# A dilated 3x3 convolution on one core: the first pair of images loaded in one transfer, casts two groups ahead, and stores and a load moved in the queue

## The chip, the core and the metric

The kernel runs on one core of a Trainium2 chip. The metric is device time in microseconds (us) of one execution, lower is better; the median of several runs is given. A profile was taken of one execution. Its engines are PE (matrix products), DVE (vector), ACT (scalar), POOL, and SP, whose queue here issues every transfer between the chip's main memory and the on-chip buffers; the transfers themselves run on 16 DMA engines.

## The reference

Sixteen images of 64 channels and 64x64 pixels (f32) are convolved with a 3x3 kernel of dilation 2 into 128 output channels, with zero padding of 2, so that the output is again 64x64.

```
x: (16, 64, 64, 64) f32      weight: (128, 64, 3, 3) f32      output: (16, 128, 64, 64) f32
output[b, co] += weight[co, ci, kh, kw] * x_pad[b, ci, kh*2 : kh*2+64, kw*2 : kw*2+64]   for all ci, kh, kw
```

So 16.8 MB are read and 33.6 MB are written.

## The kernel before

**Tiles.** The images are taken in pairs: two images of 64 channels fill the 128 partitions, 16 KB of f32 to a partition, 2048 KB to a pair. There are `npairs` = 8 pairs. A pair is worked through in `NG` = 4 groups of 16 rows, so the main loop (L174) runs over 32 groups; `G` counts them all, `pb` is the pair, `g` the group within it. The output of a pair is two images of 2048 KB, kept in one tile `osb` until it is stored.

**Arithmetic.** Rows are grouped by twos, and with dilation 2 the sum over the three kernel rows is rearranged so that two blocks of output share one product. Five kinds of derived weights (`w_sb`, made from `w32` by casts, differences and transposes through PE in `turn`, L116) are used. In each group PE makes three PSUM results: `psP` from `xs` (sums of neighbouring row blocks, 6 matmuls), `psA` and `psB` from `x16` (12 matmuls each). ACT copies `psP` to `p_sb` (L201), and DVE adds `p_sb` to `psA` and to `psB` into `osb` (L206).

**Staging.** `load(pb)` (L60) queues a transfer of a pair into an `x32` tile, of which there are 3. `cast(c)` (L67) is ACT's conversion of one group's rows to f16 (`x16`, 2 tiles of a pair each); it takes rows up to two past its group, since the group's products read two rows ahead. `rowsum(c)` (L77) is DVE's making of `xs`. `osb` has 3 tiles, `p_sb` 3, PSUM one buffer for `psP` and three that `psA` and `psB` share.

**Order.** The order on each engine is the program's: nothing is rescheduled. On SP's queue stand the weights (L86), pair 0 in four pieces (rows 0 to 10, 10 to 18, 18 to 34 and 34 to 64, L87), pairs 1 and 2, and then, from the loop, `load(3)` after group 0 and the two stores of pair 0 after group 3, `load(4)` after group 4, the stores of pair 1 after group 7, and so on. `load(pb + 3)` has to wait until the last cast of pair `pb` has freed the `x32` tile. A wait on SP holds up everything behind it on that queue. The last pair is stored in half images after groups 1 and 3 (L216).

**Ahead of the loop** the rows of group 0 are cast by hand: rows 0 to 10 by ACT (L132), rows 10 to 18 by DVE (L135), then `rowsum(0)` (L139). Between them stand the copies of the five transposed weight kinds from PSUM to `w_sb`: DVE L131, ACT L138, DVE L142, ACT L143, DVE L144. In the loop, `cast(G + 1)` stands after the matmuls of `psP` (L187) and `rowsum(G + 1)` after ACT's copy (L202).

Of the kernel before, what the change touches and what calls it, by code (L numbers as in the profile page):

```python
# [10 lines left out]
def kernel(  # L11
# [9 lines left out]
    B, CI, H, W = x.shape  # L21
# [5 lines left out]
    d = 2  # L27
# [8 lines left out]
    GR = 16  # L36
    NG = H // GR
    NBLK = GR // 4
    NH = GR // 2 * W
    npairs = B // 2  # L40
    ngroups = npairs * NG
# [18 lines left out]
    def load(pb, cuts=(0, H)):  # L60
        x32_tiles[pb] = fpool.tile([P, HW], f32, tag="x32", name="x32")
        for lo, hi in zip(cuts[:-1], cuts[1:]):
            nc.sync.dma_start(  # L63
                out=x32_tiles[pb][:, lo * W : hi * W], in_=x_pair[pb, :, lo * W : hi * W]
            )

    def cast(c):  # L67
        pb, g = divmod(c, NG)
        lo, hi = chunk_rows[g]
        if g == 0:  # L70
            x16_tiles[pb] = xpool.tile([P, HW], f16, tag="x16", name="x16")
            xs_tiles[pb] = xpool.tile([P, HW // 2], f16, tag="xs", name="xs")
        nc.scalar.copy(  # L73
            out=x16_tiles[pb][:, lo * W : hi * W], in_=x32_tiles[pb][:, lo * W : hi * W]
        )

    def rowsum(c):  # L77
        pb, g = divmod(c, NG)
        v = x16_tiles[pb][:, g * GR * W : (g + 1) * GR * W].rearrange(
            "p (b e q) -> p b e q", e=2, q=2 * W  # L80
        )
        s = xs_tiles[pb][:, g * NH : (g + 1) * NH].rearrange("p (b q) -> p b q", q=2 * W)
        nc.vector.tensor_tensor(out=s, in0=v[:, :, 0], in1=v[:, :, 1], op=add)  # L83

    w32 = wpool.tile([CO, CI * KH * KW], f32, name="w32")
    nc.sync.dma_start(out=w32, in_=weight.rearrange("o i h w -> o (i h w)"))  # L86
    load(0, (0, 10, GR + d, 2 * GR + d, H))  # L87
    load(1)
    load(2)
    zero = wpool.tile([P, 512], f16, name="zero")  # L90
# [55 lines left out]
    def product(ps, src, kind, blk0, nblk, first, last):  # L146
        for j in (1, 0, 2):
            dw = (j - 1) * d
            o0, o1 = max(0, -dw), W - max(0, dw)
            t = kind * KW + j  # L150
            for hb in range(2):
                pp = slice(hb * CI, (hb + 1) * CI)
                rhs = src(pp, dw + o0, dw + o1)
                po = ps[:, hb * NH + blk0 * 2 * W : hb * NH + (blk0 + nblk) * 2 * W]
                po = po.rearrange("p (r w) -> p r w", w=W)[:, :, o0:o1]
                nc.tensor.matmul(  # L156
                    out=po,
                    lhsT=w_sb[pp, t * CO : (t + 1) * CO],
                    rhs=rhs,
                    start=first and j == 1,  # L160
                    stop=last and j == 2,
                )

    def blocks(x16, b0, n, e):
        v = x16.rearrange("p (b e r w) -> p b e r w", e=2, r=2, w=W)
        return lambda pp, c0, c1: v[pp, b0 : b0 + n, e, :, c0:c1]

    def store(pb, m, r0=0, r1=H):
        nc.sync.dma_start(
            out=out_img[2 * pb + m, :, r0 * W : r1 * W],  # L170
            in_=o_tiles[pb][:, m * HW + r0 * W : m * HW + r1 * W],
        )

    for G in range(ngroups):  # L174
        pb, g = divmod(G, NG)
        x16 = x16_tiles[pb]
        xs = xs_tiles[pb].rearrange("p (r w) -> p r w", w=W)
        if g == 0:
            o_tiles[pb] = opool.tile([P, 2 * HW], f32, tag="osb", name="osb")
        o = o_tiles[pb].rearrange("p (m b e q) -> p m b e q", m=2, e=2, q=2 * W)  # L180
        b0 = g * NBLK

        psP = ppool.tile([P, 2 * NH], f32, tag="p", name="psP")
        sv = lambda pp, c0, c1: xs[pp, g * GR // 2 : (g + 1) * GR // 2, c0:c1]
        product(psP, sv, 0, 0, NBLK, True, True)

        if G + 1 < ngroups:  # L187
            cast(G + 1)

        psA = apool.tile([P, 2 * NH], f32, tag="ab", name="psA")  # L190
        product(psA, blocks(x16, b0, NBLK, 1), 1, 0, NBLK, True, False)
        z = 1 if g == 0 else 0
        product(psA, blocks(x16, b0 + z - 1, NBLK - z, 1), 2, z, NBLK - z, False, True)

        psB = apool.tile([P, 2 * NH], f32, tag="ab", name="psB")
        product(psB, blocks(x16, b0, NBLK, 0), 3, 0, NBLK, True, False)
        z = 1 if g == NG - 1 else 0
        product(psB, blocks(x16, b0 + 1, NBLK - z, 0), 4, 0, NBLK - z, False, True)

        p_sb = spool.tile([P, 2 * NH], f32, tag="psb", name="p_sb")  # L200
        nc.scalar.copy(out=p_sb, in_=psP)  # L201
        if G + 1 < ngroups:  # L202
            rowsum(G + 1)
        pv = p_sb.rearrange("p (m b q) -> p m b q", m=2, q=2 * W)
        for e, ps in ((0, psA), (1, psB)):
            nc.vector.tensor_tensor(  # L206
                out=o[:, :, b0 : b0 + NBLK, e],
                in0=ps.rearrange("p (m b q) -> p m b q", m=2, q=2 * W),
                in1=pv,
                op=add,  # L210
            )

        if g == NG - 1 and pb < npairs - 1:
            store(pb, 0)
            store(pb, 1)
        if g % 2 == 1 and pb == npairs - 1:  # L216
            store(pb, 0, (g - 1) * GR, (g + 1) * GR)
            store(pb, 1, (g - 1) * GR, (g + 1) * GR)
        if g == 0 and pb + 3 < npairs:
            load(pb + 3)  # L220


# [33 lines left out]
```

## Time and profile before

| | us |
|---|---|
| median of 5 runs (128.08 to 130.51) | 129.08 |
| the profiled execution, its time | 129.52 |
| its span, from first to last instruction | 127.7 |
| last instruction of DVE ends | 109.5 |
| PE, DVE, ACT busy | 104.6, 91.2, 65.1 |

A page of the profile gives the busy time of each engine, the load of the DMA engines in 40 equal slices of the span, the chain of work that ended last, the costliest groups of instructions and the DMA issues. Besides it the trace answers questions: a table by stretches of time (busy time of each engine, granted PE clock, share of the 16 DMA engines, GB/s), a timeline of instructions, waits by engine, and the landing times of transfers. "L156" is line 156 of the kernel.

### The profile page before, as it was taken

To read this page: it belongs to the slowest core of one execution; us is meant where nothing else is said; L and a number is where in the kernel's file an instruction comes from. 1 tells how busy PE (TensorE), PEld (TensorE's weight loads), DVE (VectorE), ACT (ScalarE), POOL (GpSimd) and SP (SyncE) were. 2 spreads that over 40 slices of the span, in tenths; PEclk is the share of its full clock that TensorE was granted. 3 is DMA by queue.
4 is the path that set the end of the run, shared out by engine and by line. 5 is a ranking of instruction groups with operands and counts; after the bars stand their busy time and mean duration, and the time that the engine had idled before them with its cause. 6 is when DMAs were issued, how large, how long until landed. Compare 5 with 4: busy or idle time off the path is not lost.

```text
span 127.7 us, 2334 instructions
## 1 busy us (share of the span) xinstructions
PE 104.6 (82%) x996; PEld 48.4 (38%) x996; DVE 91.2 (71%) x103; ACT 65.1 (51%) x68; POOL 2.2 (2%) x8
## 2 busy tenths in 40 slices
PE   6669999999999999999999999999999998000000
PEld 2324444444444444444444544444444443000000
DVE  0556888988898889888888988898889887300000
ACT  4555566656665666566656665665666533000000
POOL 2400000000000000000000000000000000000000
PEclk9968999999999999999999999999999999975555
DMA  4999999999999999999999999999999999999980
GB/s 140 274 403 460 431 410 421 395 416 446 364 369 323 426 436 423 426 421 441 426 421 428 431 431 421 436 431 431 426 431 426 431 426 431 426 413 421 426 341 21
DMA packets 4330, 50.78 MB, mean 398 GB/s; under 512 B 480, under 2 KB 480, under 8 KB 1120
## 3 DMA queue, kind: packets, MB, share of 16 engines
q1 hardware_dynamic: 4320, 50.63, 95.7%
q8 instruction: 8, 0.13, 0.4%
q14 instruction: 2, 0.02, 0.0%
HBM read 17.07 MB, written 33.55 MB: 396 GB/s over the span
## 4 chain that ended last, share of the span: by engine, by line
PE 78%; DMA 4%; DVE 2%; DVEq 1%; SPq 1%; issue 0%
PE psA L156 32%; PE psB L156 30%; PE psP L156 17%; DMA x<-in_x_dram 4%; DVE osb L206 1%; DVEq L251 1%; DVE x L135 0%; DVE xs L83 0%; SPq L63 0%; SPq L86 0%; DVEq L206 0%; DVEq L83 0%
## 5 line engine op out<-in xcount | busy, mean ns | idle before, releaser
L156 PEld LDWEIGHTS <-w_sb 64*128 64x128 f16 x960 | 46.7, 95 | 55.1 <-issue 1.9
L201 ACT COPY p_sb<-psP 128x1024 f32<-128x1024 f32 x32 | 32.4, 1012 | 36.5 <-issue 31.9
L206 DVE TENSOR_TENSOR osb<-psA,p_sb 128x1024 f32<-128x1024 f32 x32 | 39.2, 1225 | 12.6 <-PE psA L156 11.8
L156 PE MATMUL psA<-x,w_sb 64*128 64x496 f16 (+3 forms) x384 | 45.5, 371 | 0.0
L156 PE MATMUL psB<-x,w_sb 64*128 64x496 f16 (+3 forms) x384 | 44.5, 365 | 0.0
L206 DVE TENSOR_TENSOR osb<-psB,p_sb 128x1024 f32<-128x1024 f32 x32 | 39.1, 1222 | 0.0
L73 ACT CAST x<-x 128x1024 f16<-128x1024 f32 (+2 forms) x31 | 32.4, 1044 | 0.3 <-DMA x<-in_x_dram 0.3
L156 PE MATMUL psP<-xs,w_sb 64*128 64x496 f16 (+1 forms) x192 | 26.1, 379 | 1.3 <-DVE xs L83 1.3
L83 DVE TENSOR_TENSOR xs<-x 128x512 f16<-128x512 f16 x32 | 13.3, 416 | 1.2 <-ACT x L73 1.1
L98 PE MATMUL dm<-zero 128*128 128x512 f16 x6 | 2.7, 630 | 1.2 <-DVE zero L91 1.2
L108 DVE CAST wd<-w 128x192 f16<-128x192 f32 x1 | 0.5, 500 | 2.5 <-DMA w<-in_weight_dram 2.5
L121 PE MATMUL wt<-ident,wd 128*64 128x128 f16 x30 | 1.2, 221 | 1.0 <-DVE w_sb L131 0.8
L121 PEld LDWEIGHTS <-wd 128*64 128x64 f16 x30 | 1.0, 109 | 2.0 <-DVE wd L108 1.1
L110 ACT ACT_TABLE_LOAD x1 | 1.3, 1283 | 0.7 <-PEq L237 0.7
L98 PEld LDWEIGHTS <-zero 128*128 128x128 f16 x6 | 0.7, 138 | 2.3 <-DVE zero L91 1.2
L143 ACT CAST w_sb<-wt 128x384 f16<-128x384 f32 x1 | 0.5, 478 | 1.8 <-DVE w_sb L142 1.8
L110 ACT CAST wd<-w 128x192 f16<-128x192 f32 x1 | 0.5, 537 | 1.6 <-DMA w<-in_weight_dram 1.6
L135 DVE CAST x<-x 128x512 f16<-128x512 f32 x1 | 0.4, 427 | 1.2 <-DMA x<-in_x_dram 1.2
L132 ACT CAST x<-x 128x640 f16<-128x640 f32 x1 | 0.7, 725 | 0.6 <-DMA x<-in_x_dram 0.6
L91 DVE MEMSET zero<- 128x256 uint32 x1 | 0.3, 272 | 0.9 <-PEq L237 0.9
L109 POOL TENSOR_TENSOR wd<-w 128x192 f16<-128x192 f32 x1 | 0.8, 793 | 2.3 <-DMA w<-in_weight_dram 2.3
L112 POOL CAST wd<-w 128x192 f16<-128x192 f32 x1 | 0.8, 810 | 0.0
(11 smaller groups left out, 3.8 us busy)
## 6 DMA issues: line engine op xcount, KB each, us to landing
out_dram<-osb SPq DMA_DIRECT2D x14, 2048.0 KB, 17.0
x<-in_x_dram SPq DMA_DIRECT2D x7, 2048.0 KB, 17.1
out_dram<-osb SPq DMA_DIRECT2D x4, 1024.0 KB, 16.5
x<-in_x_dram SPq DMA_DIRECT2D x1, 960.0 KB, 8.1
x<-in_x_dram SPq DMA_DIRECT2D x1, 512.0 KB, 6.3
x<-in_x_dram SPq DMA_DIRECT2D x1, 320.0 KB, 3.6
w<-in_weight_dram SPq DMA_DIRECT2D x1, 288.0 KB, 2.8
x<-in_x_dram SPq DMA_DIRECT2D x1, 256.0 KB, 4.8
```

Source lines behind the costliest of these rows:

```text
L73: nc.scalar.copy(out=x16_tiles[pb][:, lo * W : hi * W], in_=x32_tiles[pb][:, lo * W : hi * W])
L83: nc.vector.tensor_tensor(out=s, in0=v[:, :, 0], in1=v[:, :, 1], op=add)
L98: nc.tensor.matmul(out=dm[:, 0:512], lhsT=zero[:, 0:P], rhs=zero)
L109: nc.gpsimd.tensor_tensor(out=wdv[:, 3], in0=wv[:, 0], in1=wv[:, 1], op=sub)
L110: nc.scalar.copy(out=wdv[:, 2], in_=wv[:, 0])
L112: nc.gpsimd.tensor_copy(out=wdv[:, 4], in_=wv[:, 2])
L121: nc.tensor.matmul(out=wts[k // 2][r * CI : (r + 1) * CI, c0 + j * CO : c0 + (j + 1) * CO], lhsT=wd[:, t * CI : (t + 1) * CI], rhs=ident,)
L132: nc.scalar.copy(out=x16_tiles[0][:, 0 : 10 * W], in_=x32_tiles[0][:, 0 : 10 * W])
L156: nc.tensor.matmul(out=po, lhsT=w_sb[pp, t * CO : (t + 1) * CO], rhs=rhs, start=first and j == 1, stop=last and j == 2,)
L201: nc.scalar.copy(out=p_sb, in_=psP)
L206: nc.vector.tensor_tensor(out=o[:, :, b0 : b0 + NBLK, e], in0=ps.rearrange("p (m b q) -> p m b q", m=2, q=2 * W), in1=pv, op=add,)
L251: with _tile.TileContext(nc) as tc:
```

## The change

Four things are done.

- Pair 0 is loaded in one transfer, like the other pairs, in place of four pieces. The hand-made casts of rows 0 to 10 and 10 to 18 stay as they are.
- `cast` runs two groups ahead: group 0 issues `cast(1)` and `cast(2)`, and each later group `G` issues `cast(G + 2)`.
- `load(pb + 3)` is queued in group 1 of pair `pb` in place of group 0, and ahead of that group's stores.
- Pair 0 is stored in half images after groups 1 and 3, as the last pair already is, in place of whole images after group 3.

```
-    load(0, (0, 10, GR + d, 2 * GR + d, H))
+    load(0)
...
-        if G + 1 < ngroups:
-            cast(G + 1)
+        if G == 0:
+            cast(1)
+        if G + 2 < ngroups:
+            cast(G + 2)
...
-        if g == NG - 1 and pb < npairs - 1:
+        if g == 1 and pb + 3 < npairs:
+            load(pb + 3)
+        if g == NG - 1 and 0 < pb < npairs - 1:
             store(pb, 0)
             store(pb, 1)
-        if g % 2 == 1 and pb == npairs - 1:
+        if g % 2 == 1 and pb in (0, npairs - 1):
             store(pb, 0, (g - 1) * GR, (g + 1) * GR)
             store(pb, 1, (g - 1) * GR, (g + 1) * GR)
-        if g == 0 and pb + 3 < npairs:
-            load(pb + 3)
```

## The prediction

> **What bounds the kernel now.** I read the page first, then the table by stretches, SP's timeline, and the first 12 us of the timeline. From the page:
>
> ```profile
> DMA  4999999999999999999999999999999999999980
> ...
> q1 hardware_dynamic: 4320, 50.63, 95.7%
> ...
> PE 78%; DMA 4%; DVE 2%; DVEq 1%; SPq 1%; issue 0%
> ```
>
> The chain of waits names PE, but it ends with DVE's last addition at 109.5 us, 18 us before the span does. The DMA row stands at 9 or 8 in 38 of 40 slices. The table by stretches (busy PE, PEld, DVE, ACT, POOL, then clock, DMA share, GB/s) prices that:
>
> ```profile
> 1.70:4.00 2.30, 2.23 (x6) 0.49 (x4) 0.40 (x1) 0.71 (x2) 0.35 (x1) 1.00 1.02 272
> 4.00:8.00 4.00, 1.71 (x34) 1.22 (x36) 2.67 (x7) 1.38 (x4) 1.19 (x2) 0.91 0.95 329
> ...
> 22.50:24.00 1.50, 1.50 (x18) 0.76 (x16) 1.33 (x3) 1.50 (x2) 0.00 (x0) 1.00 0.79 339
> ...
> 32.00:40.00 8.00, 8.00 (x84) 3.78 (x80) 7.00 (x9) 5.43 (x6) 0.00 (x0) 1.00 1.01 344
> 40.00:109.50 69.50, 68.18 (x662) 31.75 (x658) 61.32 (x67) 41.14 (x42) 0.00 (x0) 1.00 1.01 428
> 109.50:123.00 13.50, 0.00 (x0) 0.00 (x0) 0.04 (x1) 0.00 (x0) 0.00 (x0) 0.63 0.99 422
> ```
>
> The steady rate is 428 GB/s; 50.63 MB at that rate are 118.3 us, so the queue of transfers is the bound and compute ends early. The queue falls short three times. From 1.7 to 8 us, with pair 0's small pieces, it moves 1.94 MB in 6.3 us, which want 4.5: 1.8 us lost. Around 23 us pair 0's stores come too late: 0.3 us. From 32 to 40 us it is busy but slow: 2.75 MB, which want 6.4 us: 1.6 us lost. There packets of every direction take up to twice their usual 0.61 us, and at no later pair again, so I take it for a disturbance of this execution. The runs agree: 129.52 - 1.6 is about the fastest (128.08). SP's timeline says what is queued when:
>
> ```profile
> 0.73 0.37 SPq L86 DMA_DIRECT2D w<-in_weight_dram  x1
> 1.16 13.96 SPq L63 DMA_DIRECT2D x<-in_x_dram  x7
> 22.98 0.82 SPq L169 DMA_DIRECT2D out_dram<-osb  x2
> 27.20 0.34 SPq L63 DMA_DIRECT2D x<-in_x_dram  x1
> 35.35 0.81 SPq L169 DMA_DIRECT2D out_dram<-osb  x2
> ```
>
> The issue view for `load(4)`, issued at 27.20, says that it takes 15.6 us, so it lands at 42.8, well after pair 1's stores were queued at 35.35: from there on the queue never runs dry.
>
> ```profile
> x<-in_x_dram SPq DMA_DIRECT2D x1, 2048.0 KB, 15.6
> ```
>
> From that landing to the end of the span are 127.7 - 42.8 = 84.9 us, all of it transfers at full rate and a tail of about 1 us after the last landing (126.8). Nothing in the change touches this stretch. So the question is only when pair 1's first store packets start.
>
> **The skill.** "DMA: Bandwidth & Descriptors", Where 436 GB/s comes from, states a ceiling of 435 GB/s for the 16 engines; the trace's 428 agrees, so no reordering can pass it. Its section Queues, rings and completion order says that a transfer's 16 shares finish independently, so a waiter waits for the slowest: the trace agrees (the shares of `load(4)` land from 40.6 to 42.8). "TensorE: Matmul & The Clock Gate", Part 1, says that PE's clock halves after an idle window of some 3.4 us, windows run free, and a busy window restores it; in the trace the clock is 0.50 from 7.3 to 10.6 us, which agrees.
>
> **The change, part by part.** One 2048 KB transfer takes 2.10 MB / 428 = 4.9 us.
>
> *Pair 0 in one transfer.* Removed: three of four issues (0.43 us each on SP, in no one's way) and small packets. The first compute now waits for all of pair 0. Before, it ran so:
>
> ```profile
> 4.75 0.72 ACT L132 CAST x<-x 128x640 f16<-128x640 f32 x1 [0.62 <-DMA x<-in_x_dram]
> ...
> 6.49 0.43 DVE L135 CAST x<-x 128x512 f16<-128x512 f32 x1 [1.22 <-DMA x<-in_x_dram]
> 7.03 0.43 DVE L83 TENSOR_TENSOR xs<-x 128x512 f16<-128x512 f16 x1
> ...
> 7.51 1.44 PE L156 MATMUL psP<-xs,w_sb 64*128 64x512 f16 x6 [1.33 <-DVE xs L83]
> ```
>
> The weights' packets end at about 3.1 us. Then 4.9 us of data, and about 0.6 for a start-up slower than steady and for the landing: 8.6. Bounds: 8.0 (no such costs) and 10.7, when the fourth piece landed before (960 KB, issued at 2.6, 8.1 us), had the small pieces cost nothing. From 8.6: L132 0.72 on ACT beside L135 on DVE, to 9.4; `rowsum(0)` 0.43, to 9.85; PE starts at 9.95 against 7.51, 2.4 late. What was covered before now stands behind these casts. On ACT: the copy L138 (0.48, to 9.85), L143 after DVE's L142 (to 11.0), `cast(1)` 1.04 to 12.0 and, new, `cast(2)` 1.04 to 13.1 ahead of the copy of `psP`, which ends at 14.1. On DVE: L142 and L144, 0.55 each, to 11.0.
>
> PE: cold matmuls cost 1.44/6 = 0.24, warm 0.106. It goes cold at 7.3 as before; starting at 9.95 it leaves the window that ends near 10.7 mostly idle, so I take the next, near 14.1, for the warming: 4.1 us cold in place of 3.1, 0.5 us of work lost (lower bound 0: the phase of the windows is unknown). So `psP` 10.0 to 11.4, `psA` to 14.15, which also covers ACT's copy (to 14.1), `psB` to 15.4, against 12.24: **compute is 3.2 us late** (2.4 to 5.3 with the landing's bounds). From there PE's pitch of about 3.1 us a group is unchanged, so it stays late by that.
>
> *Casts ahead.* Cover, not work: 31 casts as before. The waits show DVE's `rowsum` waiting for ACT's cast once, 1.1 us, in group 0. In later groups nothing waits for a cast. Worth 0, besides the 1.04 above, and an earlier free `x32` tile: `cast(3)` follows the copy of group 0, 14.1 to 15.05, so `load(3)` is issued at 15.1 (before: 14.8).
>
> *Load a group later.* `load(4)`: `cast(7)` now stands ahead of group 5's copy, done at about 27.4, so it is queued at about 27.4 as before (27.2), behind pair 0's second half store. Every later load is likewise where it was, and lands far ahead of its cast. 0 us.
>
> *Half stores of pair 0.* Two more issues (0.4 us each, SP is idle then), the same bytes. First halves after group 1: 16.68 + 3.2, so queued at 19.9; second halves at 22.98 + 3.2 = 26.2. From issue to first byte is about 0.95 us (weights: 0.73 to 1.7).
>
> *The queue in sum.* Pair 0 through at 8.1; loads 1, 2, 3 at 13.0, 17.9, 22.8 (`load(3)` ready at 16.1, no gap); first halves to 27.7 (ready at 20.9: the 0.3 us gap is gone); second halves to 32.6 (ready at 27.2: 0.5 us in hand); `load(4)` to 37.5. **Pair 1's stores are queued at 35.35 + 3.2 = 38.55, first packet 39.5: the queue is empty for 2.0 us.** That is the new stall; what follows (`load(5)` and pair 2's stores at 51) is in time, since a pair takes 14.7 us of transfers and 12.4 of compute. All 16 engines restart together at 39.5; before, the slowest started pair 1's stores at 42.3 (landing 42.8 less 0.45). Gain 2.8 us. Check: 1.8 + 0.3 + 1.6 saved or absorbed, 2.0 paid, is 1.7 on average over engines; the slowest engine, which sets the end, gains 1.1 more because the empty queue lets it catch up. The span is 39.5 + 0.45 + 84.9 = 124.9; with the 1.8 us that lie around it, **126.7**. To the profiled 129.52 that is -2.8, to the median 129.08 it is -1.8%.
>
> **Rivals.**
>
> *Early arrival* (0.18): the clock's phase is kind and pair 0 lands at 8.0. Compute is 1.8 to 2.4 late, restart at 38.1 to 38.7: 125.3 to 125.9. For it: the lower bounds; against it: two must meet.
>
> *Hardly any change* (0.25): either pair 0 lands near 10.7, compute is 5.3 late, restart at 41.6, 128.8; or a disturbance of 1.6 us comes after the restart, where no gap absorbs it: 126.7 + 1.6 = 128.3. For it: the first 2 us of transfers are slow whatever their size, perhaps; the runs before show such disturbances in about half.
>
> *Slower* (0.07): PE stays cold. The place is pair 1's store, L169; each us of late compute beyond the 2.0 before the queue is dry costs one. Slower by 1% (130.4) needs a restart at 43.2, compute 6.9 late: 3.7 more than forecast, or more than two further windows at half clock, 1.7 us each. Against it: from 10 us on PE is fed without a break.
>
> *The change doesn't do what it says*: the casts ahead have nothing to hide; this is in the forecast at 0.
>
> **Chances and range.** The forecast's own case has 0.5, at 126.7, own range 126.0 to 127.7. About 1% is what a measurement of this kernel can tell from no change: faster below 127.8, slower above 130.4. Faster: 0.5 + 0.18, 0.68; same 0.25; slower 0.07. Range 125.2 to 128.8, from the early arrival to the upper end of the third case.
>
> **What would show it.** `L132` starting at 8.0 to 9.0 us; PE's first `psP` at about 10; a first load phase near 428 GB/s; no gap at 23; the DMA row broken just once, at 37.5 to 39.5, ahead of pair 1's stores; last DVE addition at about 112.7; the span 85.4 us longer than the first packet of those stores. It is wrong if there is no break there, if one comes at 15 to 17 or 26 to 28 us (`load(3)` or second halves late), or if the small pieces were not what slowed the first 8 us.

## The result, and the profile after

The changed kernel takes 129.48 us (median of 43 runs, 128.61 to 130.75); the kernel before, with more runs by then, 129.62 us (80 runs, 127.37 to 130.96). The ratio is 1.0063, with a 95% interval of 1.0042 to 1.0084; it leaves out runs more than 1.5% above the fastest of the same kernel, which are 52 of the 80 runs of the kernel before and one of the changed kernel, and so stands above 1 where the medians stand level. That is no difference that matters, and not the 126.7 us that were forecast. The profiled execution took 130.34 us, its span is 128.5.

The page of the changed kernel, the three lines that answer to those shown of before:

```profile
DMA  6999999999996999999999999999999999999991
...
q1 hardware_dynamic: 4176, 50.63, 95.4%
...
PE 79%; DMA 6%; DVE 1%; DVEq 1%; ACT 1%; SPq 0%; issue 0%
```

The DMA row starts at 6 in place of 4, and has a 6 in the middle, in slice 13, which is the empty queue that was forecast. SP's timeline of the changed kernel gives the queue:

```profile
1.17 13.82 SPq L63 DMA_DIRECT2D x<-in_x_dram  x4
20.59 7.08 SPq L169 DMA_DIRECT2D out_dram<-osb  x4
28.08 0.55 SPq L63 DMA_DIRECT2D x<-in_x_dram  x1
39.24 0.81 SPq L169 DMA_DIRECT2D out_dram<-osb  x2
```

Pair 1's stores are queued at 39.24, 3.9 us later than before (35.35). The table by stretches of the changed kernel (columns as in the prediction's table, the last is GB/s):

```profile
1.70:4.00 2.30, 2.23 (x6) 0.49 (x4) 0.34 (x1) 0.65 (x2) 0.29 (x1) 1.00 1.04 306
4.00:8.00 4.00, 2.02 (x30) 1.67 (x30) 1.35 (x3) 0.20 (x1) 1.26 (x2) 1.00 1.02 434
38.00:40.00 2.00, 2.00 (x24) 0.98 (x22) 1.83 (x4) 1.43 (x2) 0.00 (x0) 1.00 0.20 82
40.00:48.00 8.00, 8.00 (x80) 3.70 (x76) 7.17 (x8) 4.52 (x6) 0.00 (x0) 1.00 1.00 424
48.00:50.50 2.50, 2.50 (x30) 1.18 (x26) 2.08 (x4) 1.89 (x2) 0.00 (x0) 1.00 1.12 347
50.50:53.00 2.50, 2.50 (x28) 1.25 (x26) 1.93 (x3) 1.85 (x2) 0.00 (x0) 1.00 0.94 387
53.00:56.00 3.00, 3.00 (x32) 1.36 (x28) 2.91 (x4) 2.04 (x2) 0.00 (x0) 1.00 1.07 306
56.00:109.50 53.50, 53.50 (x520) 25.19 (x518) 47.48 (x53) 31.30 (x33) 0.00 (x0) 1.00 1.01 428
```

From 4 to 8 us the queue now runs at its full rate (before: 329). From 38 to 40 the DMA engines' busy share is 0.20: 1.6 of 2.0 us are empty. And then, with the queue full again and that share at 1.1, it is slow twice, at 347 and 306 GB/s with 387 between, where the kernel before ran at 428 on average. In what follows, a slow stretch is such a time: the engines are busy, but packets take longer and fewer bytes move.

A transfer is spread over the 16 engines, and each engine's part of it, called a share below, lands for itself. When each transfer's middle share (the 8th of 16) landed shows where the gain went. These are the completion records of the profiled executions; the last kernel is that of experiment e14 below:

```
landed, us                before   changed   difference   e14
pair 0 (its last piece)     9.3      8.6       -0.8       8.4
load(3)                    23.9     23.2       -0.7      24.0
pair 0's last store        34.8     33.8       -1.0      34.1
load(4)                    40.8     38.9       -1.9      38.7
pair 1's first store half
 or image                  45.7     45.4       -0.3      43.6 (2 half images)
pair 1's last store        50.9     51.0       +0.1      48.7
load(5)                    55.4     57.2       +1.8      53.4
pair 2's last store        65.4     67.1       +1.7      63.3
last store, middle share  124.2    125.6       +1.4     122.8
last store, last share    126.8    127.5       +0.7     125.2
```

Up to `load(4)` the changed kernel gains 1.9 us. The next transfer gives 1.6 of it back, the empty queue. The next two lose about 2 more with the engines busy. From there on the two kernels run alike. The gain up to `load(4)` is also less than was forecast: `load(4)` was to be through at 37.5, and its middle share landed at 38.9, which is 38.4 without the 0.45 us of the landing. A part of that is one more slow stretch, ahead of the empty queue, at the end of pair 0's stores:

```profile
32.00:34.00 2.00, 2.00 (x22) 0.91 (x20) 1.58 (x3) 1.61 (x2) 0.00 (x0) 1.00 1.03 311
```

### The profile page after: what moved, and what is told of

Same layout as the page of the kernel before. It is cut to its first block, busy times and chain, and to the rows that moved or that the text cites. A ratio compares the mean times of both kernels' runs of the same rounds, so it can differ in the third digit from the quotient of the medians.

```text
span 128.5 us, 2326 instructions
## 1 busy us (share of the span) xinstructions
PE 106.8 (83%) x996; PEld 49.8 (39%) x996; DVE 91.2 (71%) x103; ACT 64.9 (51%) x68; POOL 2.2 (2%) x8
## 4 chain that ended last, share of the span: by engine, by line
PE 79%; DMA 6%; DVE 1%; DVEq 1%; ACT 1%; SPq 0%; issue 0%
PE psA L156 31%; PE psB L156 31%; PE psP L156 16%; DMA x<-in_x_dram 6%; DVE osb L208 1%; DVEq L253 1%; ACT x L132 1%; DVE xs L83 0%; SPq L86 0%; DVEq L208 0%
## 5 line engine op out<-in xcount | busy, mean ns | idle before, releaser
L156 PEld LDWEIGHTS <-w_sb 64*128 64x128 f16 x960 | 47.4, 96 | 57.6 <-issue 3.6
L156 PE MATMUL psB<-x,w_sb 64*128 64x496 f16 (+3 forms) x384 | 45.8, 372 | 0.0
L83 DVE TENSOR_TENSOR xs<-x 128x512 f16<-128x512 f16 x32 | 13.3, 416 | 1.4 <-ACT x L73 1.0
L121 PE MATMUL wt<-ident,wd 128*64 128x128 f16 x30 | 2.0, 311 | 1.0 <-DVE w_sb L131 0.7
L121 PEld LDWEIGHTS <-wd 128*64 128x64 f16 x30 | 1.7, 165 | 2.0 <-DVE wd L108 1.2
L111 DVE TENSOR_TENSOR wd<-w 128x192 f16<-128x192 f32 x1 | 0.8, 799 | 0.0
## 6 DMA issues: line engine op xcount, KB each, us to landing
out_dram<-osb SPq DMA_DIRECT2D x8, 1024.0 KB, 10.1
```

The costliest lines, as they stand in the source:

```text
L111: nc.vector.tensor_tensor(out=wdv[:, 1], in0=wv[:, 2], in1=wv[:, 1], op=sub)
L121: nc.tensor.matmul(out=wts[k // 2][r * CI : (r + 1) * CI, c0 + j * CO : c0 + (j + 1) * CO], lhsT=wd[:, t * CI : (t + 1) * CI], rhs=ident,)
L156: nc.tensor.matmul(out=po, lhsT=w_sb[pp, t * CO : (t + 1) * CO], rhs=rhs, start=first and j == 1, stop=last and j == 2,)
```

## The experiments

In what follows "A", "B" and "C" are the theories named in the first expectation. Where a kernel moves data alone, it says what is left out.

**e1: four pieces again.** The changed kernel with `load(0, (0, 10, GR + d, 2 * GR + d, H))` in place of `load(0)`.

> The changed kernel with pair 0 in four pieces again (the rest of the change kept). Compute is then on time and the queue is never empty: pair 0's first halves are queued at about 16.7 us, the second at 23.0, load(4) at 27.2, pair 1's stores at 35.4, while load(4)'s data last until 38. Theory A (an empty queue brings the 16 engines into step; from some 9 us after the restart stretches of slow packets follow, about 2 us in all): no slow stretch, span about 125.8, time about 127.6, ratio to the kernel before 0.985. Theory B (a slow stretch of 1.6 to 2 us comes once in every execution, whatever the queue does): span about 127.4, time 129.2, ratio 0.997. Theory C (the slow stretch belongs to the first pair that is stored in whole images and the load behind it): as B, with the slow packets after pair 1's stores, near 46 to 52 us.

Measured: 128.35 us (9 runs; before 129.28), ratio 0.9915 (0.9889 to 0.9942); the profiled span is 127.1. The queue is never empty. This is about midway between A and B. A said no slow packets, but the queue was slow at 51 to 54 (347 GB/s), close behind where C had it. So e1 alone decides for none of the three. It shows that the rest of the change is worth about 1% alone, and that it was the single load that took it.

**e2: the single load alone.** The kernel before with `load(0)`.

> The kernel before with pair 0 loaded in one transfer and nothing else of the change. Compute is 3 to 4 us late, pair 0's stores are queued at about 26.9, first packet 27.8, while load(3) is through at 22.9: the queue is empty for about 4.9 us. A: slow stretches 9 and 13 us after the restart (near 37 and 41), span about 129.6, time 131.4, ratio 1.014. B: a slow stretch at any place, and none more for the empty queue: 127.9 to 129.6, ratio 1.000 to 1.014. C: as A.

Measured: 132.35 us (6 runs), ratio 1.0203 (1.0154 to 1.0251). The table by stretches of this kernel:

```profile
24.00:28.00 4.00, 4.00 (x44) 1.90 (x40) 3.83 (x5) 2.37 (x3) 0.00 (x0) 1.00 0.47 201
36.00:38.00 2.00, 2.00 (x24) 0.95 (x20) 1.88 (x2) 0.94 (x2) 0.00 (x0) 1.00 1.00 328
40.00:43.00 3.00, 3.00 (x32) 1.36 (x30) 2.58 (x4) 1.85 (x2) 0.00 (x0) 1.00 1.08 295
```

The queue is half empty from 24 to 28, and slow at full share 9 and 13 us after it fills again, as A said. It also ran low earlier, which was not forecast: `load(3)` was issued only at 17.95, when `cast(3)`, not ahead in this kernel, had freed its tile (share 0.67 and 139 GB/s at 17.5 to 19.5). That is the one thing that casting two groups ahead is seen to be worth: with the single load it keeps `load(3)` at 14.7.

**e3 and e4: transfers alone.** The loads and stores in the order of before, each pair in its own buffer, no compute; in e4 one store takes its data from the tile that `load(4)` has just filled:

```
+        src = xt[4] if (pb, m) == (1, 0) else osb[:, m * HW : (m + 1) * HW]
+        nc.sync.dma_start(out=out_img[2 * pb + m], in_=src)
```

> Transfers alone, in the order of the kernel before, none of which waits (every pair has its own buffer; the convolution is left out, the stores write a constant). The queue is never empty. A: no slow stretch, every 16 KB packet near 0.61 us; span 118.3 us of bytes at 428 GB/s, and 1.7 before and some 2 to 3 after: 122 to 123. B: 1.6 to 2 us more, 124 to 125, with packets of over 1 us on all engines for 2 to 4 us. C: as B, with the slow packets in pair 0's second store and load(4).

> The same transfers alone, but pair 1's first store takes its data from the tile that load(4) fills, so it waits for that landing and the queue is empty once, for about 1.4 us near 38 (the convolution is left out). A: 1.4 us and slow stretches of 1.6 to 2 us, 9 and 13 us after the restart: 3.0 to 3.4 us more than without the wait. B and C: 1.4 us more, no new slow stretch.

Measured: 125.63 us (4 runs) and 128.56 (8 runs); spans 124.3 and 126.8. The tables by stretches (DVE, POOL, clock, DMA share, GB/s), first e3:

```profile
48.00:50.50 2.50, 0.00 (x0) 0.00 (x0) 1.00 1.01 433
...
53.00:56.00 3.00, 0.00 (x0) 0.00 (x0) 1.00 1.01 431
```

then e4:

```profile
38.00:40.00 2.00, 0.00 (x0) 0.00 (x0) 1.00 0.04 16
...
48.00:50.50 2.50, 0.00 (x0) 0.00 (x0) 1.00 1.05 315
...
53.00:56.00 3.00, 0.00 (x0) 0.00 (x0) 1.00 1.02 300
```

The same order of transfers, with no compute in sight, is slow at 48 to 56 if the queue ran empty at 38 to 40, and not otherwise. The places and rates are nearly those of the changed kernel (347 and 306). Between the medians lie 2.9 us for a spell of less than 2. B falls as it stood: where such stretches come depends on the program. So does C: in e3 pair 0's whole images and `load(4)` pass at full rate. A isn't whole either: e3, never empty, has one slow stretch, late in the last of four loads ahead of the first store (e4 has it too, also at 322 GB/s):

```profile
20.00:23.00 3.00, 0.00 (x0) 0.00 (x0) 1.00 1.07 322
```

**e5: the kernel before, profiled again.**

> The kernel before, unchanged, profiled once more. Theory A (slow packets follow a restart of the queue, here the gap of up to 0.9 us at 23): slow packets again at about 33 and 37 to 39, some 1.5 us in all, and nowhere else. Theory B (a disturbance from outside): at another place, or none and a span of about 126.

Measured: 128.70 us, span 126.9. One slow stretch, where A expected it, but half as long, and it came although the queue had no gap at 23 in this execution (426 GB/s from 22.5 to 24):

```profile
36.50:39.00 2.50, 2.50 (x28) 1.12 (x26) 2.09 (x3) 1.85 (x2) 0.00 (x0) 1.00 1.07 341
```

So the slow packets that the prediction took for a disturbance of one execution come again at 36.5 to 39 in the second profile of this kernel: they go with the program, and an empty queue isn't the only thing that brings them.

**e6: half stores of pair 0 alone**, on the kernel before.

```
-        if g == NG - 1 and pb < npairs - 1:
+        if g == NG - 1 and 0 < pb < npairs - 1:
...
-        if g % 2 == 1 and pb == npairs - 1:
+        if g % 2 == 1 and pb in (0, npairs - 1):
```

> The kernel before with pair 0 stored in half images and nothing else of the change. The gap at 23 us goes; compute and loads are as before. A: the slow stretch that followed the gap shrinks as in the changed kernel with four pieces (from 1.5 to 1.1 us or less), span about 126.5, ratio to the kernel before 0.991. B: only the gap's 0.3 us, ratio 0.998.

Measured: 128.13 us (22 runs; before 129.28), ratio 0.9965 (0.9936 to 0.9994); the profiled span is 126.3. The ratio agrees with B, the span with A. In the profiled execution the slow stretch of before is gone:

```profile
32.00:40.00 8.00, 8.00 (x82) 3.82 (x80) 7.00 (x9) 5.72 (x6) 0.00 (x0) 1.00 1.03 435
```

It is e1's time within the runs' scatter (128.35), so casts ahead and the moved load add nothing to it that these runs show.

**e7: PE kept busy while pair 0 lands.** The changed kernel with `dummies(10)` after `t4 = turn(4)`.

> The changed kernel with ten idle matmuls put after the last transposes, so that PE isn't idle while pair 0 lands. PE's clock is then full when group 0 starts; compute is 1.3 to 1.6 us earlier than in the changed kernel, pair 1's stores are queued at about 37.7, first packet 38.6, and the empty queue (1.6 us) shrinks to 0.0 to 0.4. A: the slow stretch at 48 to 56 (1.9 us) shrinks too: span 125.5 to 126.8, ratio to the kernel before 0.98 to 0.99. B: only the empty time: span about 127.2, ratio 0.996.

Measured: 128.52 us (14 runs, 128.35 to 128.76), ratio 0.999 (0.9964 to 1.0016); the profiled span is 126.9. Pair 1's stores were queued at 37.10, 2.1 us earlier, and the empty spell is gone. But the time is B's rather than A's: the span lies just above A's 125.5 to 126.8, near B's 127.2, and the ratio is even above B's 0.996. A slow stretch like that of e3 appeared at 20 to 23 (pair 0's stores, queued earlier too, now stood behind `load(3)` while it ran; that this is the reason isn't shown). And the one after 48 us did not go with the empty spell:

```profile
20.00:23.00 3.00, 3.00 (x32) 1.65 (x30) 2.58 (x4) 1.95 (x2) 0.00 (x0) 1.00 1.00 279
38.00:40.00 2.00, 2.00 (x22) 1.06 (x20) 2.00 (x3) 0.84 (x2) 0.00 (x0) 1.00 1.00 426
48.00:50.50 2.50, 2.50 (x28) 1.39 (x26) 1.93 (x4) 1.70 (x2) 0.00 (x0) 1.00 0.91 387
52.00:54.00 2.00, 2.00 (x22) 1.12 (x20) 1.91 (x3) 1.88 (x2) 0.00 (x0) 1.00 0.99 262
```

From 48 to 56 it moves 387, 387 and 325 GB/s over the three stretches of the changed kernel's table, a loss of 1.2 us against 428, where the changed kernel loses 1.6.

**e8: what the slow stretch is tied to.** e4 with four stores and then two loads behind the empty spell.

> Transfers alone with the one empty spell near 38 us, but behind it four stores and then two loads in place of two stores and a load (the convolution is left out). If slow packets come at a set time after the restart: at 49 and 53 to 55 us as with two stores, then in the middle of the third and fourth store. If they come where stores give way to a load while the 16 engines are in step: about 10 us later, near 59 and 63 to 65. If they were neither: none.

Measured: one run, span 126.4. The table by stretches:

```profile
48.00:50.50 2.50, 0.00 (x0) 0.00 (x0) 1.00 1.00 419
53.00:56.00 3.00, 0.00 (x0) 0.00 (x0) 1.00 1.03 437
58.00:60.50 2.50, 0.00 (x0) 0.00 (x0) 1.00 1.12 328
67.00:70.00 3.00, 0.00 (x0) 0.00 (x0) 1.00 1.06 333
```

No set time: the stretches moved to the end of the fourth store, just ahead of the loads, and to the second load, ahead of the next stores; the first load was clean. The second stretch was expected at 63 to 65, in the first load, and came a load later. So in this one run packets were slow ahead of a change between storing and loading, once in each direction after the restart.

**e9 to e11 and e13: do the engines have to be in step?** After the restart at 40 us all 16 engines go together: the shares of the changed kernel's next store land within 0.2 us (45.4 to 45.6). e9 is e3 with pair 0 in four pieces, which spreads their landings over 2.0 us (9.1 to 11.0; 0.5 us in e3). e10 is e4, and e11 the changed kernel, with pair 1's first image stored as partitions 0 to 112, 112 to 120 and 120 to 128, the last two over 8 engines; e13 is e4 with two extra stores of 8 rows, every sixteenth partition, behind it.

> Transfers alone as before, never waiting, but pair 0 in four pieces (the convolution is left out). Theory A2 (packets slow ahead of a change between loads and stores when the 16 engines are in step): the pieces spread the engines by 1 to 2 us in the first 8 us, so the slow packets at 20 to 23 (1.1 us with one transfer) shrink to 0.4 or less; the pieces cost about 0.8 to 1.8 at the start, so the span is within 1 us of that with one transfer (124.3). If the step of the engines has no part in it: 1.1 us of slow packets at 20 to 23 again, span 125 to 126.

> Transfers alone with one empty spell, but the first store behind it is cut by partitions into 112, 8 and 8: the last two go over 8 engines each, so that after it 8 engines stand about 1.2 us behind the other 8 (the convolution is left out). A2: the slow stretches at 49 and 53 to 55 (1.75 us) go nearly away (under 0.5), at a price of 0.6 us for the uneven load: span 125.3 to 126.2, against 126.8. If the step of the engines has no part in it: the same 1.75 us of slow packets, span 127.4.

> The changed kernel with pair 1's first image stored in cuts of 112, 8 and 8 partitions, the same bytes. A2: the slow packets at 48 to 56 (1.9 us) shrink to under 0.6, 0.6 us is paid for the uneven load: about 0.7 to 1.0 us faster than the changed kernel, ratio to the kernel before 0.995 to 1.000. If the step has no part in it: 0.6 us slower than the changed kernel, ratio 1.010.

> Transfers alone with one empty spell; behind it, after pair 1's first store, two extra stores of 8 rows each (every sixteenth partition, to a spare place in main memory) that go over 8 engines, so that these stand 1.2 us behind the other 8, without the slow rows that the cuts of 8 neighbouring partitions had (the convolution is left out). If slow packets ahead of a change of direction need engines in step: under 0.5 us of them at 48 to 57 in place of 1.75, span 126.0 to 126.5. If not: 1.75 us again, span 128.0.

Measured: e9 126.85 us (4 runs), span 125.8; at 20 to 23 it moves 399 GB/s where e3 moved 322. The slow stretch shrank as A2 said, but the span missed by 0.5 us what A2 allowed. e10 134.56 (4 runs), e11 135.60 (6 runs; ratio 1.0485, 1.0438 to 1.0531), e13 132.34 (1 run): all far outside either forecast. The stores of 8 rows were slow themselves (in e13 packets of 16 KB took 1.5 to 2.7 us against 0.61 while they ran), and set engines far more than 1.2 us apart (the shares of pair 1's next store land over 3.9 us in e13 and over 6.5 us in e11). Slow packets still came ahead of the following change (336 GB/s at 54 to 58 in e13, a loss of 0.9 us). The step of the engines is not shown to be the cause: e9 fits it, the others rather speak against it.

**e12: the changed kernel, profiled again.**

> The changed kernel, unchanged, profiled once more. A2: the queue is empty at about 38 to 40 again and slow packets follow before the changes of direction near 50 and 56, some 1.5 to 2 us. If they came from outside: at another place or none.

Measured: 129.92 us, span 128.1; 147 GB/s at 38 to 40, 288 at 48 to 50.5, 300 at 53 to 56. The same places as in the first profile, which a chance from outside would not choose.

**e14: the empty spell taken away, compute left alone.** The changed kernel with pair 1 stored in halves too.

```
-        if g == NG - 1 and 0 < pb < npairs - 1:
+        if g == NG - 1 and 1 < pb < npairs - 1:
...
-        if g % 2 == 1 and pb in (0, npairs - 1):
+        if g % 2 == 1 and pb in (0, 1, npairs - 1):
```

> The changed kernel with pair 1 stored in half images too, so that the queue has pair 1's first halves from about 33 us on and is never empty; compute stays 3.9 us late. The empty spell (1.6 us at 38 to 40) goes. If slow packets follow the restart: those at 48 to 56 (1.9 us) shrink to 1 or less as well, span 125.5 to 126.5, ratio to the kernel before 0.982 to 0.992. If only the empty time counts: span 126.9, ratio 0.994.

Measured: 127.87 us (10 runs; before 129.30), ratio 0.9907 (0.9873 to 0.9941); the profiled span is 126.1. Pair 1's first halves are queued at 31.64. Its table by stretches:

```profile
38.00:40.00 2.00, 2.00 (x22) 0.93 (x20) 1.83 (x3) 1.10 (x2) 0.00 (x0) 1.00 0.93 393
...
48.00:50.50 2.50, 2.50 (x32) 1.27 (x28) 2.50 (x3) 1.44 (x2) 0.00 (x0) 1.00 1.07 455
...
53.00:56.00 3.00, 3.00 (x32) 1.36 (x30) 2.91 (x4) 1.89 (x3) 0.00 (x0) 1.00 0.98 418
```

With the empty spell, both slow stretches after 48 us are gone. The one of e3 and e7 is there:

```profile
20.00:23.00 3.00, 3.00 (x32) 1.38 (x30) 2.75 (x3) 1.74 (x3) 0.00 (x0) 1.00 1.10 333
```

In this execution PE's clock was full at 13.3, so compute was only 2.6 us late, and about 1.3 of the 1.6 us of the empty spell would have gone by that alone; but its other runs took no longer (mean clock below 0.93: median 127.95 of 4, above 0.95: 127.87 of 4). It is faster than the kernel before by 0.9%, and its median is 1.6 us below that of the changed kernel. Whether the single load pays in it isn't shown: four pieces with halves of both pairs were not tried, and e1, with four pieces and halves of pair 0 alone, is 0.5 us slower but was measured at another time.

## Why the prediction was wrong

- **DMA queue as the bound: right.** The changed kernel's steady rate is again 428 GB/s and its compute ends at 113.4 us, 15 us before the span does.
- **Single load, 1.8 us saved: right in kind, smaller.** By 8 us the changed kernel has moved 0.306 x 2.3 + 0.434 x 4 = 2.44 MB against 1.94, worth 1.2 us; pair 0's last share landed at 8.8 (forecast 8.6, before 10.7).
- **Compute 3.2 us late: 3.9.** The start was as worked out:

```profile
8.83 0.73 ACT L132 CAST x<-x 128x640 f16<-128x640 f32 x1 [4.62 <-DMA x<-in_x_dram]
...
10.07 1.44 PE L156 MATMUL psP<-xs,w_sb 64*128 64x512 f16 x6 [3.17 <-DVE xs L83]
```

  PE's clock was full only at 15.9, where the forecast took 14.1. When that comes differs from execution to execution, and with it the mean clock: 17 of 44 executions have more than 0.95 and a median of 128.80, 13 have 0.945 to 0.95 and 130.09, and 14 have less and 129.60. Both profiles of the changed kernel (130.34 and, in e12, 129.92) are of the second kind, so what is said here of the sizes holds for its slower executions; none of the quicker was profiled. e7, where PE was kept busy, has all its runs between 128.35 and 128.76. So PE's clock seems to set the time of the changed kernel, in that it sets when the queue runs dry; that is argued from these averages.
- **Casts ahead, later load: 0 in the sum.** Right by e1 against e6, as far as their scatter tells. The forecast's "earlier free `x32` tile" is what e2 shows: without the casts ahead, the single load holds `load(3)` up.
- **Half stores: the gap at 23 gone.** Nearly: the share at 22.5 to 24 is 0.89 in the changed kernel and 0.93 in e6, against 0.79 before; e6 has the gain alone.
- **An empty queue of 2.0 us, restart at 39.5: right in kind.** It was 1.6 us, with the restart at about 40.2 (39.24 and 0.95 us from issue to first byte), since compute and `load(4)` were both later than forecast.
- **The step that failed:** "From that landing to the end of the span are 127.7 - 42.8 = 84.9 us, all of it transfers at full rate [...] Nothing in the change touches this stretch", with "I take it for a disturbance of this execution". From 40.2 + 0.45 to the end of the span are 87.8 us in the changed kernel, 2.9 too many; with the restart 0.7 late that is the 3.6 us between 124.9 and 128.5. The slow packets of before at 33 to 39 went with the program (e5 has some of them too), ahead of 42.8 and so outside the 84.9. In the changed kernel a slow stretch falls into it, after the restart: at 48 to 56 the table's rates stand for some 1.6 us (347, 387 and 306 GB/s against 428 over 2.5, 2.5 and 3.0 us). e4 makes the same with no compute, from an empty spell alone; in e14 it is gone with the empty spell, in e7 only a quarter of it is.
- **"The empty queue lets it catch up", 1.1 us: didn't last.** Right after the restart no share was behind (45.4 to 45.6), but at the end of the changed kernel the last one lands 1.9 us behind the middle one again (127.5 and 125.6). Before, it was 2.0 behind at `load(4)` (42.8 and 40.8) and 2.6 at the end, so that it fell back by only 0.6. The difference, 1.3 us, is the rest of the 2.9.
- **The rival "hardly any change" held, by another way** than either of its two: it had a disturbance of 1.6 us after the restart as a chance from outside. A loss of that size came, but in both profiles at the same place (e12), and by e4 as a consequence of the empty spell.

Open: why packets slow ahead of a change between storing and loading. With transfers alone an empty spell is enough to bring it on (e4 against e3). It isn't needed (e3, e5, e7, and the changed kernel itself at 32 to 34), and taking it away removed the slow stretch once (e14) and in the main not once (e7). That engines in step are the reason was tried in four runs and not shown.

## What to carry to other kernels

When transfers are the bound, what counts is that the queue never runs dry, and a dry spell can cost up to about twice its length, since transfers behind it may run slow for a while (here 1.6 us empty and 1.6 us lost behind it). Before a first load is made larger, work out when the first stores will be ready against when the loads queued ahead of them are through; store early pieces (halves of the first two pairs here) so that the queue has something to do. And a slow stretch in one profile should not be called a disturbance until a second profile lacks it.

## What the runs showed of the hardware that was not expected

- At full queue, many 16 KB packets took 0.9 to 1.25 us in place of 0.61 for 1 to 3 us ahead of a change between stores and loads (changed kernel, 48 to 56 us); with transfers alone too (300 to 333 GB/s in e3, e4 and e8).
- While stores of 8 rows over 8 engines ran, packets of 16 KB took 1.5 to 2.7 us (e13). Cutting one image's store so made e11 slower than the kernel before by 5% (ratio 1.0485), though it moves the same bytes.
- PE's clock became full 3.2 us after the loop's first matmul in the profile of before (10.7 against 7.5) and 5.8 us after it in that of the changed kernel (15.9 against 10.1).
